# Split weights at drawn places in their buffers, and a narrower array of shifted columns

## The chip, the cores and the metric

The kernel runs on one core of one Trainium2 chip, in one launch. The metric is device time in microseconds. The kernel before was timed three times: 2295.11, 2295.64 and 2296.51 us, a median of 2295.64 us. Lines of the profile name the engines: PE is TensorE (matmuls), PEld its weight loads, DVE is VectorE, ACT is ScalarE, POOL is GpSimd, and SP is the engine that issues most DMAs.

## The reference

Two layers of a decoder trunk on one sequence of 256 tokens with 2048 channels, in float32. Each layer has a token mixer (layer 0 a causal convolution module, layer 1 stick-breaking attention with 16 heads) and a gated feed-forward part with a causal convolution of width 3. Every part is normalised and modulated by shift, scale and gate, which are products of the conditioning vector with a weight matrix of its own:

```python
def ada_ln(c, w, b):
    mod = jax.nn.silu(c) @ w + b
    shift, scale, gate = jnp.split(mod, 3, axis=-1)
    return shift[:, None, :], scale[:, None, :], gate[:, None, :]
...
def conv_ffn(h, up_w, dw_w, dw_b, down_w):
    u = causal_depthwise_conv(h @ up_w, dw_w, dw_b)
    gt, val = jnp.split(u, 2, axis=-1)
    return (jax.nn.silu(gt) * val) @ down_w
...
    for i in range(DEPTH):
        j = i // N_MIXERS
        shift, scale, gate = ada_ln(c, mix_mod_w[i], mix_mod_b[i])
        h = rms_norm(x, mix_norm_g[i]) * (1.0 + scale) + shift
        if i % N_MIXERS == 0:
            y = conformer_conv_module(h, cv_pw1_w[j], cv_pw1_b[j], cv_dw_w[j], cv_dw_b[j],
                                      cv_ln_g[j], cv_ln_b[j], cv_pw2_w[j], cv_pw2_b[j])
        else:
            y = stick_breaking_mixer(h, sb_qkv_w[j], sb_o_w[j])
        x = x + gate * y
        shift, scale, gate = ada_ln(c, ffn_mod_w[i], ffn_mod_b[i])
        h = rms_norm(x, ffn_norm_g[i]) * (1.0 + scale) + shift
        x = x + gate * conv_ffn(h, ffn_up_w[i], ffn_dw_w[i], ffn_dw_b[i], ffn_down_w[i])
    return rms_norm(x, final_norm_g)
```

`D_FF` is 5632, so the two up and down projections, the four products of the attention (q, k, v, o) and the two of the convolution module (pw1, pw2) are nearly all of the arithmetic.

## The kernel before

Activations are kept transposed: channels on the 128 partitions, the 256 tokens along the free dimension, 16 tiles for 2048 channels. All weight matrices but the modulation's come in pieces of 8 blocks of 128x128 (`PB`, `PW` = 1024 columns, 4096 bytes in a partition), in the order in which a table (`plan`) uses the blocks.

**Split weights.** Except for pw1, a product is made in the faster float32r type with each factor split into a high part and a low rest. A piece is loaded by SP into one of 6 `raw` buffers (`load_next`, L231), ACT copies it with rounding into `wh` (L241), and DVE subtracts that from the piece into `wl` (L245). `wh` and `wl` have 4 buffers each in the pool `wsplit`, one behind the other, and three pieces are split ahead of the one in use. Each 128x128 block is 512 bytes in a partition.

**Products.** `gemm` walks through the pieces. For each block it issues either three matmuls of 256 columns, high with high, high with low, low with high (L301, L302, L303), or two: the high weights against high and low part of the activations side by side, 512 columns (L296), and the low weights against the high part, 256 columns (L297). The second way is taken where `both` is given: in all of the second layer's up projections but the first four tiles, in the attention's o and its q and k but the first four tiles, and in the down projections, save for the last of their 16 output tiles. In `v_product` the roles change: the activations are the weights that are loaded, and the split weights stream through, 512 columns in each of L1184 to L1186.

**Where activations lie.** `h_tiles` places the 16 tiles of h 2304 bytes apart, the low part 1056 bytes behind the high part (a gap of 32 bytes). `halved` does so for the other split activations by the table `PAIRS`: the second layer's g like h, the first layer's g and o 2048 bytes apart and without a gap, z 2112 bytes apart with a gap of 32 bytes. The first tile can be moved by an offset (`ahead`).

**Order.** Each engine executes its instructions in program order. The order of pieces comes from `plan`; the work of ACT and DVE between the matmuls is placed by rates per piece (`RATES`). The change edits `split_next`, and two places of the first part that take it up: `load_rows` (L556, three of its row tiles lie in buffers of `wsplit`) and `hot`.

**The array of shifted columns.** In the first part, `mod_rows` makes some of the modulation vectors with rows of the matrix as the moving operand. The weights there are 32 columns of `hot`, all zero but one: `hot` holds silu(c) at column 31 of 63 for each of 16 tiles (L525 to L527), and the slice `31 - i : 63 - i` puts it at column `i` (L585). `i` is 0 to 3.

Of the kernel before, what the change touches and what calls it, by code (L numbers as in the profile page):

```python
# [2 lines left out]

# [7 lines left out]
F32 = mybir.dt.float32  # L11
F32R = mybir.dt.float32r
# [4 lines left out]
P = 128  # L17
PB = 8
PW = PB * P
# [99 lines left out]
def hybrid_trunk(ctx: ExitStack, tc: tile.TileContext, cfg: Cfg, io: dict):  # L119
    nc = tc.nc  # L120
    D, T, H = cfg.D, cfg.T, cfg.H
    KD, KF, CW, FW = cfg.KD, cfg.KF, cfg.CW, cfg.FW
# [7 lines left out]
    w_pool = ctx.enter_context(tc.tile_pool(name="wsplit", bufs=4))  # L130
# [5 lines left out]
    def psum_acc():  # L136
        return acc.tile([P, 512], F32, name="ps")
# [4 lines left out]
    def psum_b():  # L142
        return aux.tile([P, 512], F32, name="auxb", bufs=2)
# [22 lines left out]
    def pc(name, i0=0, n=None):  # L166
        if name in cfg.ccols:
            t, (a, b) = cpar["t"], cfg.ccols[name]
        else:
            t, (a, b) = par, cfg.cols[name]  # L170
        return t[:, a:b] if n is None else t[:, a + i0:a + i0 + n]
# [50 lines left out]
    def load(src, dst):  # L222
        tc.keep_in_program_order(nc.sync.dma_start(dst, src))

    def load_next():
# [4 lines left out]
        load(io["w_" + name][i, :, :n], v[:, :n])  # L230
        raws.append((blocks, v, n))  # L231

    def split_next(later=False):

        blocks, v, n = raws[len(parts)]
        if stream[len(parts)][0] == "pw1":
            parts.append((blocks, v, None))
            return
        wh = w_pool.tile([P, PW], F32R, name="wh")
        wl = w_pool.tile([P, PW], F32R, name="wl")  # L240
        nc.scalar.copy(wh[:, :n], v[:, :n])  # L241
        parts.append((blocks, wh, wl))

        def low():
            nc.vector.tensor_tensor(wl[:, :n], v[:, :n], wh[:, :n].bitcast(F32), op=ALU.subtract)  # L245

        if later:
            return low
        low()

    def pieces(name):

        for i in range(-(-len(cfg.plans[name]) // PB)):
            at = look["at"]
            assert stream[at] == (name, i)
            look["at"] += 1
            while len(raws) < min(len(stream), at + 1 + look["load"]):
                load_next()
            while len(parts) < min(len(stream), at + 1 + look["split"]):
                split_next()  # L260
            yield parts[at]
# [242 lines left out]
    with ExitStack() as cv:  # L504
        cpool = cv.enter_context(tc.tile_pool(name="conv", bufs=1))
# [11 lines left out]
        for k in range(0, D, 512):  # L517
            ps = psum_acc()
# [3 lines left out]

        cs = cpool.tile([P, KD], F32, name="cs")
        nc.scalar.activation(cs, pc("c"), AF.Silu)
        hot = cpool.tile([P, KD, 63], F32, name="hot")  # L525
        nc.vector.memset(hot, 0.0)
        nc.vector.tensor_copy(hot[:, :, 31:32], cs.unsqueeze(2))  # L527

        def gate_done():
            nc.vector.tensor_tensor(gb, modv["mix0"][:, 2 * KD:3 * KD], pc("pw2_b"), op=ALU.mult)  # L530
# [13 lines left out]
        def load_rows(most=1):  # L544

            while row_chunks and most:
                n = nrow["n"]
                near = n < nrow["near"]
                home = row_homes[n] if near else ("zmm"[n % 3] if n < 8 * KD // 4 else "zm"[n % 2]) if "z" in cpar else "m"
                cap = {"m": 3 if near else 1 + (n < 8 * KD // 4), "r": MORE_ROWS, "w": SPLIT_ROWS, "z": 1}[home]  # L550
                if sum(t[1] == home for t in row_tiles) >= cap:
                    break
                m, c, k0 = row_chunks.pop(0)
                src = io["mr_" + m][mr_at[m].index(c), :, k0 * 512:(k0 + 4) * 512]
                if home == "w":
                    v = [w_pool.tile([P, PW], F32R, name=x).bitcast(F32) for x in ("wh", "wl")]  # L556
                    for i in range(2):
                        load(src[:, i * PW:(i + 1) * PW], v[i])
                    v = [v[g // 2][:, g % 2 * 512:(g % 2 + 1) * 512] for g in range(4)]
                else:  # L560
                    v = (cpool2.tile([P, 4 * 512], F32, name="mrow", bufs=MORE_ROWS) if home == "r" else
                         cpar["z"].tile([P, 4 * 512], F32, name="zrow") if home == "z" else
                         mpool.tile([P, 4 * 512], F32, name="mraw"))
                    if "z" in cpar:
                        nc.gpsimd.dma_start(v, src)
                    else:
                        load(src, v)
                    v = [v[:, g * 512:(g + 1) * 512] for g in range(4)]
                row_tiles.append((v, home))
                nrow["n"] += 1  # L570
                most -= 1

        def mod_rows():

            for m, c0, n, done in rows_of:
                ps = (psum_acc if m == "ffn0" and c0 else psum_a)() if n else None
                for i in range(n):  # L580
                    for k0 in range(0, KD, 4):
                        v = row_tiles.pop(0)[0]
                        first, last = i == 0 and k0 == 0, i == n - 1 and k0 + 4 >= KD
                        for g in range(4):
                            nc.tensor.matmul(ps[32 * g:32 * g + 32, :], hot[:, k0 + g, 31 - i:63 - i],  # L585
                                             v[g], start=first, stop=last,
                                             tile_position=(0, 32 * g))
                        load_rows()
                        if later and nrow["bias"]:
                            later.pop(0)()  # L590
                        if last:
                            rows = cpool.tile([P, 512], F32, name="rows")
                            nc.scalar.copy(rows, ps)
                        else:
                            yield
                if n:
                    ps2 = psum_b()

                    def turn(rows=rows, n=n, ps2=ps2):
                        for b in range(4):  # L600
                            nc.tensor.matmul(ps2[:, b * n:(b + 1) * n], rows[:, b * P:(b + 1) * P], sel[:, :n],
                                             start=True, stop=True)

                    def bias(m=m, c0=c0, n=n, ps2=ps2, done=done):
                        o = modv[m][:, c0 * 4:(c0 + n) * 4].rearrange("p (c b) -> p b c", b=4)
                        v = pc(bname[m], c0 * 4, n * 4).rearrange("p (c b) -> p b c", b=4)
                        nc.vector.tensor_tensor(o, ps2[:, :4 * n].rearrange("p (b c) -> p b c", b=4), v, op=ALU.add)
                        done()

                    later.extend([turn, bias])  # L610
                    yield
            while later:
                later.pop(0)()
                yield

        def mods0():
            first = 4 * cfg.rows0
            todo, loaded = list(range(first, KD)), []

            def reduce_loaded():  # L620
                while loaded:
                    on = last_of(nc.vector.engine)
                    mod_reduce("ffn0", *loaded.pop(0))
                    behind(on)

            def load_one():
                nb = todo.pop(0)
                loaded.append((nb, mod_load("ffn0", nb)))

            for _ in mod_rows():  # L630
                reduce_loaded()
                yield
                if ("ffn0", 1) in have and todo:
                    load_one()
                    yield
            while todo:
                load_one()
                yield
                reduce_loaded()
            reduce_loaded()  # L640
            if first < KD:
                mod_sum("ffn0", first, KD - first)
            have.add(("ffn0", 0))
            yield
# [172 lines left out]
        for i in range(KD * HEAD // PB):  # L817
            pw1_piece(next(pw1))
            if (i + 1) % (HEAD // PB) == 0:
                start_tile()  # L820
        fill.append(mods0())
        load_rows(1)
        look["load"], look["split"] = 5, 0
        load(io["params"], par)
# [23 lines left out]
        for c in range(KD + 1):  # L848
# [12 lines left out]
            for s in range(nd):  # L861
# [17 lines left out]
                if c == KD and s == 0:  # L879
                    low = split_next(later=True)  # L880
# [347 lines left out]
    for h in range(2):  # L1228
        t = slice(h * HT, (h + 1) * HT)
        nc.vector.reciprocal(rs[:, t], std[:, t])  # L1230
        v = mpool.tile([P, D], F32, name="mraw")[:, :KD * HT].rearrange("p (k t) -> p k t", k=KD)
# [105 lines left out]
def build(nc, cfg, arrays):  # L1337
    io = {k: nc.dram_tensor(f"in_{k}", v.shape, F32, kind="ExternalInput").ap() for k, v in arrays.items()}
    io["out"] = nc.dram_tensor("out_0", (cfg.KD // 2, P, 2 * cfg.T), F32, kind="ExternalOutput").ap()
    with tile.TileContext(nc) as tc:  # L1340
        hybrid_trunk(tc, cfg, io)
# [19 lines left out]
```

## Time and profile before

| | us |
|---|---|
| median of three runs | 2295.64 |
| lowest and highest | 2295.11, 2296.51 |
| the profiled execution | 2295.03 |
| its span, first to last instruction | 2293.3 |
| TensorE from the first large product of split weights to the end of the last down projection | 284 to 2280 |

The stages of the profiled execution, by the first matmul of each: pw1 from 24 us, pw2 from 284 us, the first feed-forward part from 407 us (up projection until 670, down until 784, up until 1029, down until 1155), attention until 1545, the second feed-forward part until 2280, in the same halves. The matmuls' records overlap, since they are pipelined: the time that one costs is the distance from its start to that of the next, not its duration. A row of the timeline begins with the start and the duration in us. A row of the windows view begins with the stretch and its length, then gives for each engine the busy time and the number of instructions, then the granted clock, the DMA share and GB/s; with a line given it counts that line alone. In the rows of groups the busy time of all and the mean of one in ns stand behind the count.

### The profile page before, as it was taken

How to read it: one execution, taken by the hardware profiler on the slowest of the kernel's cores; microseconds unless marked ns; L12 is line 12 of the kernel's file. 1: busy time of each engine (PE TensorE's matmuls, PEld its weight loads, DVE VectorE, ACT ScalarE, POOL GpSimd, SP SyncE). 2: the span in 40 equal slices, each digit the busy share in tenths (PEclk: the TensorE clock that was granted, in tenths of full speed). 3: DMA queues.
4: the chain of work that ended last, by engine and by line, in shares of the span. 5: the costliest groups of instructions: out<-in, count | busy, mean ns of one | idle time of the engine just before them, and what ended most of it. 6: DMA issues, size and time to landing. Idle time of an engine off the chain costs nothing.

```text
span 2293.3 us, 37838 instructions
## 1 busy us (share of the span) xinstructions
PE 2259.4 (99%) x14466; PEld 2013.9 (88%) x14466; DVE 1791.2 (78%) x2502; ACT 1218.4 (53%) x1930; POOL 411.6 (18%) x535
## 2 busy tenths in 40 slices
PE   7999999999999999999999999999999999999997
PEld 5888678999998999998898888889888888888887
DVE  7689968989998899999975655778899755777654
ACT  2056655755544455555465555657555544555553
POOL 4058713200002100003421100122000010000031
PEclk9999999999999999999999999999999999999999
DMA  9988798789899989888765555566787665666663
GB/s 396 417 337 305 272 364 348 279 299 336 334 332 347 347 316 331 338 325 306 291 192 161 167 174 174 166 192 232 238 286 283 194 192 185 192 192 185 193 191 111
DMA packets 139144, 603.16 MB, mean 263 GB/s; under 512 B 15441, under 2 KB 15569, under 8 KB 115153
## 3 DMA queue, kind: packets, MB, share of 16 engines
q1 hardware_dynamic: 120242, 464.42, 57.8%
q0 software_dynamic: 18720, 136.32, 16.2%
q8 instruction: 113, 1.85, 0.3%
q14 instruction: 69, 0.57, 0.1%
HBM read 598.58 MB, written 2.10 MB: 262 GB/s over the span
## 4 chain that ended last, share of the span: by engine, by line
PE 87%; DVE 6%; DMA 4%; ACT 1%; issue 1%; POOL 0%; DVEq 0%; SPq 0%; ACTq 0%; POOLq 0%
PE ps L296 33%; PE ps L297 17%; PE ps L302 9%; PE ps L301 9%; PE ps L303 9%; PE ps L694 5%; DMA mraw<-in_mt_mix 3%; DVE mraw L335 3%; DVE wl L245 1%; PE ps L1185 1%; PE ps L1184 1%; PE ps L1186 1%; PE ps L585 1%; DMA mraw<-in_mt_ffn 1%; DMA raw<-in_w_pw 1%
## 5 line engine op out<-in xcount | busy, mean ns | idle before, releaser
L245 DVE TENSOR_TENSOR wl<-raw,wh 128x1024 fp32r<-128x1024 f32 x688 | 848.1, 1239 | 298.7 <-ACT wh L241 294.5
L241 ACT CAST wh<-raw 128x1024 fp32r<-128x1024 f32 x688 | 719.5, 1048 | 663.2 <-PE ps L296 279.6
L296 PE MATMUL ps<-h,wh 128*128 128x512 f32 x1760 | 613.5, 394 | 0.0
L297 PE MATMUL ps<-h,wl 128*128 128x256 f32 x1760 | 488.8, 278 | 0.0
L296 PE MATMUL ps<-g,wh 128*128 128x512 f32 x1320 | 458.1, 392 | 0.0
L303 PE MATMUL ps<-h,wl 128*128 128x256 f32 (+1 forms) x1504 | 423.4, 281 | 0.0
L302 PE MATMUL ps<-h,wh 128*128 128x256 f32 (+1 forms) x1504 | 423.2, 281 | 0.0
L301 PE MATMUL ps<-h,wh 128*128 128x256 f32 (+1 forms) x1504 | 419.8, 279 | 0.0
L296 PEld LDWEIGHTS ps<-h,wh 128*128 128x128 f32 x1760 | 330.4, 188 | 76.3
L335 DVE CUSTOM_DVE_ANT_0 mraw<-mraw,csr 128x2048 f32<-128x2048 f32 x152 | 350.1, 2304 | 32.1 <-DMA mraw<-in_mt_mix 28.6
L297 PE MATMUL ps<-g,wl 128*128 128x256 f32 x1320 | 369.9, 280 | 2.3 <-DVE wl L245 2.2
L297 PEld LDWEIGHTS ps<-h,wl 128*128 128x128 f32 x1760 | 330.5, 188 | 0.2
L296 PEld LDWEIGHTS ps<-g,wh 128*128 128x128 f32 x1320 | 247.8, 188 | 54.7
L301 PEld LDWEIGHTS ps<-h,wh 128*128 128x128 f32 x1504 | 284.2, 189 | 0.1
L303 PEld LDWEIGHTS ps<-h,wl 128*128 128x128 f32 x1504 | 283.0, 188 | 0.4
L302 PEld LDWEIGHTS ps<-h,wh 128*128 128x128 f32 x1504 | 283.1, 188 | 0.1
L297 PEld LDWEIGHTS ps<-g,wl 128*128 128x128 f32 x1320 | 248.6, 188 | 4.2 <-DVE wl L245 4.2
L694 PE MATMUL ps<-h,raw 128*128 128x256 f32 x832 | 188.8, 382 | 0.0
L694 PEld LDWEIGHTS ps<-h,raw 128*128 128x128 f32 x832 | 157.8, 191 | 28.3 <-issue 6.7
L1025 POOL TENSOR_TENSOR x<-x,t 128x256 f32<-128x256 f32 x56 | 70.5, 1260 | 526.8 <-ACT t L1024 526.7
L1003 DVE SCALAR_TENSOR_TENSOR t<-t,par 128x254 f32<-128x254 f32 (+1 forms) x184 | 88.7, 482 | 46.6 <-ACT t L1000 43.7
L734 DVE SCALAR_TENSOR_TENSOR auxb<-u,cpar,auxb 128x256 f32<-128x256 f32 x297 | 121.6, 482 | 4.5 <-ACT auxb L718 3.8
(271 smaller groups left out, 2739.7 us busy)
## 6 DMA issues: line engine op xcount, KB each, us to landing
raw<-in_w_down SPq DMA_DIRECT2D x176, 512.0 KB, 4.2
mraw<-in_mt_ffn POOLq DMA_DIRECT2D x64, 1024.0 KB, 5.8
raw<-in_w_pw SPq DMA_DIRECT2D x96, 512.0 KB, 8.1
mraw<-in_mt_mix POOLq DMA_DIRECT2D x48, 1024.0 KB, 7.7
raw<-in_w_up01b SPq DMA_DIRECT2D x84, 512.0 KB, 6.3
raw<-in_w_up11b SPq DMA_DIRECT2D x84, 512.0 KB, 3.6
raw<-in_w_up00b SPq DMA_DIRECT2D x80, 512.0 KB, 5.7
raw<-in_w_up10b SPq DMA_DIRECT2D x80, 512.0 KB, 4.7
```

What stands on the lines that cost most here:

```text
L241: nc.scalar.copy(wh[:, :n], v[:, :n])
L245: nc.vector.tensor_tensor(wl[:, :n], v[:, :n], wh[:, :n].bitcast(F32), op=ALU.subtract)
L296: nc.tensor.matmul(o, wh[:, c], both[kt], start=first, stop=False, skip_group_check=True)
L297: nc.tensor.matmul(o[:, :T], wl[:, c], xh[kt], start=False, stop=left[nb] == 0, skip_group_check=True)
L301: nc.tensor.matmul(o, wh[:, c], xh[kt], start=first, stop=False, skip_group_check=halves > 0)
L302: nc.tensor.matmul(o, wh[:, c], xl[kt], start=False, stop=False, skip_group_check=halves > 0)
L303: nc.tensor.matmul(o, wl[:, c], xh[kt], start=False, stop=left[nb] == 0, skip_group_check=halves > 0)
L335: nc.vector.tensor_tensor_reduce(out=v, in0=v, in1=csr, scale=1.0, scalar=0.0, op0=ALU.mult, op1=ALU.add, accum_out=macc[:, nb:nb + 1])
L694: nc.tensor.matmul(banks[j][:, nb // KD * T:(nb // KD + 1) * T], w[:, b * P:(b + 1) * P], hf[kt], start=first, stop=left[j] == 0, skip_gro ...
L734: nc.vector.scalar_tensor_tensor(conv_ps[j], us[j % UBUFS][:, k:k + T], tap(j, k), conv_ps[j], op0=ALU.mult, op1=ALU.add)
L1003: nc.vector.scalar_tensor_tensor(y[:, s:], ps[:, :T - s], w(k), y[:, s:], op0=ALU.mult, op1=ALU.add)
L1025: nc.gpsimd.tensor_tensor(xs[nb], xs[nb], t, op=ALU.add)
```

## The change

The buffers of `wh` and `wl` become 56 columns (224 bytes) longer, and each piece starts in its buffer at an offset that is drawn: a multiple of 4 columns, 16 bytes, from 0 to 224 bytes, high and low part apart. The draws come from a generator with a fixed seed, so they are the same in each build. The blocks' order, the copies and the subtractions stay. The row tiles that borrow these buffers start at their beginning, as before. `hot` holds its column at place 3 of 35, which is enough for `i` from 0 to 3; it gives back as many bytes (16 x 28 x 4 = 1792) as the longer buffers take (8 x 224 = 1792).

What lies behind the pool `wsplit` in a partition moves by 1792 bytes, 7 x 256: the tiles of g and o among it, but not h, which lies ahead. What is allocated behind `hot` while it is there (z among it) stays where it was.

```diff
+import random
...
+    place = random.Random(1)
+
     def split_next(later=False):
...
-        wh = w_pool.tile([P, PW], F32R, name="wh")
-        wl = w_pool.tile([P, PW], F32R, name="wl")
+        wh, wl = (w_pool.tile([P, PW + 56], F32R, name=x) for x in ("wh", "wl"))
+        at = 4 * place.randrange(56 // 4 + 1)
+        wh = wh[:, at:at + PW]
+        at = 4 * place.randrange(56 // 4 + 1)
+        wl = wl[:, at:at + PW]
         nc.scalar.copy(wh[:, :n], v[:, :n])
         parts.append((blocks, wh, wl))
...
-        hot = cpool.tile([P, KD, 63], F32, name="hot")
+        hot = cpool.tile([P, KD, 35], F32, name="hot")
         nc.vector.memset(hot, 0.0)
-        nc.vector.tensor_copy(hot[:, :, 31:32], cs.unsqueeze(2))
+        nc.vector.tensor_copy(hot[:, :, 3:4], cs.unsqueeze(2))
...
-                    v = [w_pool.tile([P, PW], F32R, name=x).bitcast(F32) for x in ("wh", "wl")]
+                    v = [w_pool.tile([P, PW + 56], F32R, name=x)[:, :PW].bitcast(F32) for x in ("wh", "wl")]
...
-                            nc.tensor.matmul(ps[32 * g:32 * g + 32, :], hot[:, k0 + g, 31 - i:63 - i],
+                            nc.tensor.matmul(ps[32 * g:32 * g + 32, :], hot[:, k0 + g, 3 - i:35 - i],
```

## The prediction

> **What bounds the kernel now.** I read the busy shares first, then the waits of TensorE, then the chain that ended last.
>
> ```profile
> PE 2259.4 (99%) x14466; PEld 2013.9 (88%) x14466; DVE 1791.2 (78%) x2502; ACT 1218.4 (53%) x1930; POOL 411.6 (18%) x535
> PEclk9999999999999999999999999999999999999999
> PE 87%; DVE 6%; DMA 4%; ACT 1%; issue 1%; POOL 0%; DVEq 0%; SPq 0%; ACTq 0%; POOLq 0%
> ```
>
> TensorE is busy 99% of the span at the full granted clock and carries 87% of the chain. A busy share alone says little for pipelined matmuls, so I asked for the waits of the matmuls and of the weight loads from 450 to 2280 us.
>
> ```profile
> PE ps L297 <- DVE wl L245: 2.2, 4, 0.7
> ...
> PEld ps L297 <- DVE wl L245: 4.2, 6, 1.0
> ```
>
> The largest wait of either is 4.2 us in 1830 us. So from 450 us on nothing is late for TensorE, and the time of the kernel is the number of matmuls times the distance between their starts. The counts, from the groups of matmuls kept apart by shape (mean ns behind the busy us); they are the same in both kernels:
>
> ```profile
> L296 PE MATMUL ps<-h,wh 128*128 128x512 f32 x1760 | 613.5, 394 | 0.0
> L296 PE MATMUL ps<-g,wh 128*128 128x512 f32 x1320 | 458.1, 392 | 0.0
> L296 PE MATMUL ps<-o,wh 128*128 128x512 f32 x256 | 89.5, 392 | 0.0
> L301 PE MATMUL ps<-h,wh 128*128 128x256 f32 x1312 | 364.7, 278 | 0.0
> L302 PE MATMUL ps<-h,wh 128*128 128x256 f32 x1312 | 368.7, 281 | 0.0
> L303 PE MATMUL ps<-h,wl 128*128 128x256 f32 x1312 | 368.6, 281 | 0.0
> L301 PE MATMUL ps<-h,wh 128*128 128x258 f32 x192 | 55.0, 287 | 0.0
> L302 PE MATMUL ps<-h,wh 128*128 128x258 f32 x192 | 54.5, 284 | 0.0
> L303 PE MATMUL ps<-h,wl 128*128 128x258 f32 x192 | 54.8, 285 | 0.0
> ```
>
> I call L296 (512 columns) with its L297 (256 columns) a pair, and L301, L302, L303 (256 columns each) a triple. Both stream 768 columns; the triple loads weights three times, the pair twice. There are 1760 + 1320 + 256 pairs in these rows and 32 more whose output lies in the other banks, 3368 in all, and 1312 + 32 = 1344 triples on h of 256 columns.
>
> A matmul's record is longer than the distance to the next, so the distances come from the starts. First and last L296 of a stretch of pairs on g, and how many there are in it:
>
> ```profile
> 1809.71 0.39 PE L296 MATMUL ps<-g,wh 128*128 128x512 f32 x1
> 1909.89 0.39 PE L296 MATMUL ps<-g,wh 128*128 128x512 f32 x1
> ...
> 1810.00:1910.00 100.00, 100.00 (x290) 54.16 (x289) 1.00 0.62 191
> ```
>
> 100.18 us for 289 steps: **346.6 ns a pair**. The same for triples on h (L301, 567 of them):
>
> ```profile
> 449.78 0.28 PE L301 MATMUL ps<-h,wh 128*128 128x256 f32 x1
> 649.77 0.28 PE L301 MATMUL ps<-h,wh 128*128 128x256 f32 x1
> ...
> 450.00:650.00 200.00, 157.36 (x567) 106.88 (x566) 1.00 0.88 324
> ```
>
> 199.99 us for 566 steps: **353.3 ns a triple**. Pairs on the first layer's g, which lies differently (below):
>
> ```profile
> 679.62 0.39 PE L296 MATMUL ps<-g,wh 128*128 128x512 f32 x1
> 779.81 0.39 PE L296 MATMUL ps<-g,wh 128*128 128x512 f32 x1
> ...
> 680.00:780.00 100.00, 100.00 (x290) 54.11 (x289) 1.00 0.92 342
> ```
>
> 100.19 / 289 is 346.7 ns, the same. Two more kinds of triple, on g at the end of the first down projection (21 steps) and on z at the end of pw2 (16 steps):
>
> ```profile
> 784.20 0.28 PE L303 MATMUL ps<-g,wl 128*128 128x256 f32 x1
> 791.55 0.28 PE L303 MATMUL ps<-g,wl 128*128 128x256 f32 x1
> ...
> 401.47 0.28 PE L303 MATMUL ps<-z,wl 128*128 128x256 f32 x1
> 407.07 0.28 PE L303 MATMUL ps<-z,wl 128*128 128x256 f32 x1
> ```
>
> 7.35 / 21 and 5.60 / 16: **350.0 ns** both times. These triples have the same columns, the same weights' place and the same engine as those on h; only the place of the moving operand differs, and 3.3 ns of 353 come with it. So places matter, by about 1%, and this is the whole lever of the change.
>
> **The places, before and after.** Before, every block of split weights starts at the same place modulo 256 bytes (the pieces step 4096 bytes, the blocks 512). Let the distance be the moving operand's address minus its weights', modulo 256. Tiles of h and of the second layer's g step by a multiple of 256, so their high part is always at distance 128 and their low part at 160: pairs 346.6, triples 353.3. The first layer's g and all of o are at distance 32 in both parts: triples 350.0. Tiles of z step by 2112 bytes, 64 more than a multiple of 256, so they pass through four distances in turn: 350.0 as their mean. After, the pieces' bases step 4320 bytes and each draws 0 to 224 bytes in steps of 16. Counted over the 1312 split pieces of the changed program, each of the 16 distances in steps of 16 comes 59 to 115 times; 719 pieces (55%) lie at a multiple of 32, as all did before, and 593 (45%) at an odd multiple of 16, which no row of before shows. The order of instructions is the same, row for row, on all five engines; one MEMSET gets narrower.
>
> **The sum, term by term.**
>
> Pairs: 3368. They stand at 346.6 at both distances tried, the lowest rate in the kernel. The nearest dear row is the triple on h, 6.7 ns more for the same 768 columns; the nearest cheap one is their own. Five kinds of work are seen (pairs at two distances, triples at 32, at the four of z and at 128/160) and one of them is dear, so I let one piece in four fall to the dear rate: 6.7 / 4 = 1.7 ns on the mean, 3368 x 1.7 = +5.7 us. Ends: 0, and 3368 x 6.7 = +22.6 us.
>
> Triples on h: 1344. They hold the dear distance now and can only keep it or leave it. Three in four to the rate of z: 1344 x 3.3 x 0.75 = -3.3 us. Ends: 0 and -4.4 us.
>
> Products for v (moving operand and weights change places there, 128 of each line with the other banks) and the triples of 258 columns:
>
> ```profile
> L1184 PE MATMUL auxb<-wh,h 128*128 128x512 f32 x32 | 12.5, 392 | 0.0
> L1185 PE MATMUL ps<-wl,h 128*128 128x512 f32 x96 | 38.3, 399 | 0.0
> L1186 PE MATMUL ps<-wh,h 128*128 128x512 f32 x96 | 37.9, 394 | 0.0
> ```
>
> Equal shapes, 392 to 399 ns: if all came to 392, 9 ns x 128 = -1.2 us; if all to 399, 12 ns x 128 = +1.5 us. The 258-column triples sum to 856 ns in the rows above against 840 for 256 columns; six more columns at 353.3 / 768 ns are 2.8 ns, so 13 ns may be their place: 192 x 13 = -2.5 us at most. I take half of both gains, -1.9 us.
>
> ACT's copy and DVE's subtraction write and read the moved pieces:
>
> ```profile
> L245 DVE TENSOR_TENSOR wl<-raw,wh 128x1024 fp32r<-128x1024 f32 x688 | 848.1, 1239 | 298.7 <-ACT wh L241 294.5
> L241 ACT CAST wh<-raw 128x1024 fp32r<-128x1024 f32 x688 | 719.5, 1048 | 663.2 <-PE ps L296 279.6 <-PE ps L302 205.9 <-issue 112.4
> ```
>
> All their operands stood at one place modulo 4096, so no row says what another place costs. TensorE's lead hides a change of some per cent either way: in the fullest stage DVE is busy
>
> ```profile
> 800.00:1020.00 220.00, 220.00 (x1870) 220.00 (x1869) 204.71 (x258) 113.36 (x156) 16.41 (x31) 1.00 0.88 326
> ...
> 800.00:1020.00 220.00, 93.75 (x78) 1.00 0.88 326
> ```
>
> 204.71 of 220 us, 93.75 of them in L245 (second row), so 15.3 us are free and L245 can lengthen by 16% before DVE is the bound. I take 0.
>
> The narrow `hot` array:
>
> ```profile
> 1.25 0.90 DVE L526 MEMSET hot<- 128x1008 f32 x1 [0.16 <-issue]
> 5.58 7.31 DVE L405 TENSOR_TENSOR sumsq<-sumsq,t 128x256 f32<-128x256 f32 x14 [3.43 <-ACT t L401]
> ```
>
> 560 columns for 1008 take 0.5 us for 0.90, and DVE then waits 3.43 us for ACT anyway: 0.
>
> Sum: 5.7 - 3.3 - 1.9 = +0.5 us on 2293.3 us of span and the 1.7 us around it (the profiled execution took 2295.03): 2295.5. That execution is 0.6 us under the median of the runs, so **2296 us**, no change that can be told. A measurement of this kernel tells about 0.2%, 4.6 us, from none.
>
> The Trainium skill speaks against any effect: SBUF — State Buffer, "Who interferes with whom", gives TensorE two independent read ports and says that it waits for no one, and its remark on cachelines ("Door 1") makes 16 bytes the line, so that every draw starts on a line. By it the sum would be 0 and the time 2295.6. The rows disagree with the strong form of it: 353.3 against 350.0 ns with nothing but places different. It stays as a rival below.
>
> **The rivals.**
>
> *The pairs lose their rate (slower).* Place: L296 and L297 from 670 us on. If the 346.6 is a rate that holds only at the two distances they stand at, and others give what z gives as a mean over four, 350.0, they cost 3368 x 3.4 = +11.5 us, with the triples' gain 2302 us; if others give 353.3, +22.6 less 5 is 2313 us. For it: pairs were only seen at two distances, and 45% of the draws are of a kind not seen. Against it: the two distances differ by 96 bytes and give one rate, and z holds 350.0 over all of its four. It decides from a mean pair of 346.6 + (4.6 + 5.2) / 3368 us, 349.5 ns, on. Chance 0.33.
>
> *Most places are cheap (faster).* All pairs stay, all triples on h come to 350.0, v and the 258 columns to their cheap ends: -4.4 - 1.2 - 2.5 = -8.1 us, 2287 us. For it: four of the five kinds are at the low rate for their count of weight loads. Against it: every draw must miss the dear distance. Chance 0.23.
>
> *The change does nothing (independent ports).* Then what differs between h and z is the moving operand's own place, not its distance to the weights, and the moved weights change no rate: 2295.6 us. Against it the v rows: 392, 399 and 394 ns with the moving pieces at one place and only the h part different. Chance 0.13.
>
> *DVE or ACT slows.* At 25% on L245, 23.4 us in that stage against 15.3 free, 8.1 us; in the two stages of this kind some 17 us: 2312. Chance 0.04; nothing speaks for it but that it isn't shown.
>
> **How the numbers follow.** The forecast's own mixture has 0.27, with the independent ports 0.40 within 0.2%; the pairs and DVE give 0.37 for slower, the cheap places 0.23 for faster. The range reaches from the cheap end, 2287, to the dear end of the pairs with a little of DVE, 2315.
>
> **What would show it.** Starts of L296 over 1810 to 1910 us: 346.6 or up to 349 for the forecast, 350 and over for the first rival. Starts of L301 over 450 to 650 us: about 351 for the forecast, 353.3 for independent ports. Within a stretch the distance between pairs should now change from piece to piece, 8 pairs at a time, where before it didn't. L245 and L241 should keep 1239 and 1048 ns. I am wrong if distances at odd multiples of 16 have a rate of their own outside 346 to 353, or if TensorE begins to wait for `wl`.

## The result: 11 us slower, in the steps from pair to pair

| | before | after |
|---|---|---|
| median | 2295.64 us (2293.35 to 2301.74, 5 runs) | 2307.06 us (2305.22 to 2307.29, 5 runs) |
| ratio to before | | 1.0045, interval 1.003 to 1.006 |
| the profiled execution, and its span | 2295.03, 2293.3 | 2305.22, 2303.5 |

The changed kernel is slower by 0.45% of the time: outside the 0.2% that can be told from no change, inside the range of the prediction, and 11 us above its point. (The ratio is formed between runs that stand beside each other, so it is not quite the quotient of the medians.)

In the changed kernel the lines of the matmuls are six further down: a pair is L302 and L303, a triple L307 to L309, ACT's copy L247 and DVE's subtraction L251. From its page, the busy shares, the engines' shares of the chain that ended last, and the two groups that write and read the moved pieces:

```profile
PE 2270.5 (99%) x14466; PEld 2020.4 (88%) x14466; DVE 1791.4 (78%) x2502; ACT 1220.1 (53%) x1930; POOL 410.3 (18%) x535
...
PE 86%; DVE 7%; DMA 4%; ACT 1%; issue 1%; POOL 0%; DVEq 0%; SPq 0%; ACTq 0%; POOLq 0%
...
L251 DVE TENSOR_TENSOR wl<-raw,wh 128x1024 fp32r<-128x1024 f32 x688 | 849.0, 1240 | 308.2 <-ACT wh L247 305.9
L247 ACT CAST wh<-raw 128x1024 fp32r<-128x1024 f32 x688 | 719.6, 1048 | 673.0 <-PE ps L302 287.5
```

TensorE is still busy 99% of the span. DVE and ACT take 1240 and 1048 ns for a piece as before (1239, 1048). They merely stand idle longer, DVE 308.2 us before L251 in place of 298.7. The largest waits of the matmuls and of the weight loads from 450 us on:

```profile
PE ps L303 <- DVE wl L251: 1.7, 3, 0.7
...
PEld ps L303 <- DVE wl L251: 3.7, 6, 1.0
```

1.7 and 3.7 us, where they were 2.2 and 4.2: nothing comes late for TensorE. So what was lost lies in the matmuls themselves. Their groups by shape, for pairs and for triples on h:

```profile
L302 PE MATMUL ps<-h,wh 128*128 128x512 f32 x1760 | 619.7, 396 | 0.0
L302 PE MATMUL ps<-g,wh 128*128 128x512 f32 x1320 | 462.6, 395 | 0.0
L302 PE MATMUL ps<-o,wh 128*128 128x512 f32 x256 | 90.2, 396 | 0.0
...
L307 PE MATMUL ps<-h,wh 128*128 128x256 f32 x1312 | 368.0, 281 | 0.0
```

The counts are the same. The records of the pairs are 2 to 4 ns longer than before (394, 392 and 392), that of L307 3 ns (278). What they cost is read from the starts, in the stretches of the prediction. L302 on the second layer's g, with the window of that line:

```profile
1809.70 0.40 PE L302 MATMUL ps<-g,wh 128*128 128x512 f32 x1
1909.79 0.40 PE L302 MATMUL ps<-g,wh 128*128 128x512 f32 x1
...
1810.00:1910.00 100.00, 100.00 (x287) 53.61 (x286) 1.00 0.62 191
```

100.09 us for 286 steps are **350.0 ns a pair** (346.6 before, 290 of them in the same 100 us). On h, and then the triples on h (L307):

```profile
1599.93 0.40 PE L302 MATMUL ps<-h,wh 128*128 128x512 f32 x1
1799.89 0.40 PE L302 MATMUL ps<-h,wh 128*128 128x512 f32 x1
...
1600.00:1800.00 200.00, 200.00 (x572) 107.23 (x572) 1.00 0.73 256
```

```profile
449.77 0.28 PE L307 MATMUL ps<-h,wh 128*128 128x256 f32 x1
649.66 0.28 PE L307 MATMUL ps<-h,wh 128*128 128x256 f32 x1
...
450.00:650.00 200.00, 158.25 (x565) 106.34 (x565) 1.00 0.88 323
```

199.96 / 571 is 350.2 ns a pair; 199.89 / 564 is 354.4 ns a triple (353.3 before). The granted clock is 1.00 in all three windows, as before. Summed over all matmuls, from start to next start, after less before:

| | number | us |
|---|---|---|
| pairs on h | 1792 | +6.1 |
| pairs on the second layer's g | 660 | +2.5 |
| pairs on the first layer's g | 660 | +1.5 |
| pairs on o | 256 | +0.7 |
| triples on h, 256 columns | 1344 | +1.6 |
| triples on g; on z | | +0.3; -1.8 |
| triples of 258 columns; products for v | 192; 128 lines | -0.2; -0.5 |
| all of the matmuls | | +10.2 |

The spans differ by the same 10.2 us, so the table is all of the difference between the two traces, and the pairs are +10.8 of it. The -1.8 us on z do not come from places: in the trace of the kernel before, the granted clock was 0.50 for 3.4 us from 398.0 us on, while z was multiplied, and a triple took 640 ns there; the changed kernel's trace has no such stretch. TensorE in the same microsecond, before and after:

```profile
399.00:400.00 1.00, 1.00 (x7) 0.50 1.03 410
...
399.00:400.00 1.00, 1.00 (x11) 1.00 1.04 414
```

Of the eleven experiments' traces below, six have this stretch and five have not, whatever their places. Without it the two traces here would differ by some 12 us (an estimate: 10.2 and 1.8).

Two neighbouring pieces show how the loss of the pairs is spread, eight pairs each; rows of the timeline for the second and the last pair of the first piece, and for the first and the last of the next:

```profile
1361.97 0.40 PE L302 MATMUL ps<-h,wh 128*128 128x512 f32 x1
...
1364.17 0.40 PE L302 MATMUL ps<-h,wh 128*128 128x512 f32 x1
1364.53 0.39 PE L302 MATMUL ps<-h,wh 128*128 128x512 f32 x1
...
1366.99 0.40 PE L302 MATMUL ps<-h,wh 128*128 128x512 f32 x1
```

Six steps of the first piece take 2.20 us, 367 ns each; seven of the next take 2.46 us, 351 ns. Within these two the steps agree within some ns (elsewhere they can alternate, at 96/192 below between 345 and 365 ns), and at the boundary the rate jumps. Over all 418 pieces with at least five undisturbed steps between pairs the mean is 350.2 ns, from 341.9 to 366.7; 69 pieces, one in six, are still within half a ns of the old 346.7, or below. From here "distance" means addresses, and the time from start to start is a step or a rate. I give two distances as x/y: the address of the moving operand less that of the high weights, and less that of the low weights, both modulo 256 bytes. The first of these pieces stands at 0/32, the second at 32/96; before, h stood at 128/128 throughout.

### The profile page after: what moved, and what is told of

It is laid out like the page before. It is cut to its first block, busy times and chain, and to the rows that moved or that the text cites. A ratio compares the mean times of both kernels' runs of the same rounds, so it can differ in the third digit from the quotient of the medians.

```text
span 2303.5 us, 37838 instructions
## 1 busy us (share of the span) xinstructions
PE 2270.5 (99%) x14466; PEld 2020.4 (88%) x14466; DVE 1791.4 (78%) x2502; ACT 1220.1 (53%) x1930; POOL 410.3 (18%) x535
## 4 chain that ended last, share of the span: by engine, by line
PE 86%; DVE 7%; DMA 4%; ACT 1%; issue 1%; POOL 0%; DVEq 0%; SPq 0%; ACTq 0%; POOLq 0%
PE ps L302 32%; PE ps L303 16%; PE ps L307 9%; PE ps L308 9%; PE ps L309 9%; PE ps L700 5%; DMA mraw<-in_mt_mix 3%; DVE mraw L341 3%; DVE wl L251 2%; PE ps L1191 1%; PE ps L1192 1%; PE ps L1190 1%; PE ps L591 1%; DMA raw<-in_w_pw 1%; DMA mraw<-in_mt_ffn 1%
## 5 line engine op out<-in xcount | busy, mean ns | idle before, releaser
L251 DVE TENSOR_TENSOR wl<-raw,wh 128x1024 fp32r<-128x1024 f32 x688 | 849.0, 1240 | 308.2 <-ACT wh L247 305.9
L247 ACT CAST wh<-raw 128x1024 fp32r<-128x1024 f32 x688 | 719.6, 1048 | 673.0 <-PE ps L302 287.5
L302 PE MATMUL ps<-h,wh 128*128 128x512 f32 x1760 | 619.7, 396 | 0.0
L303 PE MATMUL ps<-h,wl 128*128 128x256 f32 x1760 | 492.8, 280 | 0.0
L302 PE MATMUL ps<-g,wh 128*128 128x512 f32 x1320 | 462.6, 395 | 0.0
L307 PE MATMUL ps<-h,wh 128*128 128x256 f32 (+1 forms) x1504 | 422.9, 281 | 0.0
L309 PE MATMUL ps<-h,wl 128*128 128x256 f32 (+1 forms) x1504 | 422.6, 281 | 0.0
L302 PEld LDWEIGHTS ps<-h,wh 128*128 128x128 f32 x1760 | 330.6, 188 | 77.0
L303 PE MATMUL ps<-g,wl 128*128 128x256 f32 x1320 | 370.1, 280 | 1.9 <-DVE wl L251 1.7
L303 PEld LDWEIGHTS ps<-h,wl 128*128 128x128 f32 x1760 | 331.8, 189 | 0.2
L302 PEld LDWEIGHTS ps<-g,wh 128*128 128x128 f32 x1320 | 247.9, 188 | 58.1
L309 PEld LDWEIGHTS ps<-h,wl 128*128 128x128 f32 x1504 | 283.5, 188 | 0.5 <-DVE wl L251 0.2
L307 PEld LDWEIGHTS ps<-h,wh 128*128 128x128 f32 x1504 | 283.5, 189 | 0.1
L303 PEld LDWEIGHTS ps<-g,wl 128*128 128x128 f32 x1320 | 248.6, 188 | 3.7 <-DVE wl L251 3.7
```

The lines of the kernel that those rows point to most:

```text
L302: nc.tensor.matmul(o, wh[:, c], both[kt], start=first, stop=False, skip_group_check=True)
L303: nc.tensor.matmul(o[:, :T], wl[:, c], xh[kt], start=False, stop=left[nb] == 0, skip_group_check=True)
L307: nc.tensor.matmul(o, wh[:, c], xh[kt], start=first, stop=False, skip_group_check=halves > 0)
L309: nc.tensor.matmul(o, wl[:, c], xh[kt], start=False, stop=left[nb] == 0, skip_group_check=halves > 0)
```

## The experiments

Theory at this point: the rate of a pair or triple follows from these two distances. Rivals: it is the draw itself, the change of place from piece to piece, that costs; it is the longer buffers and the narrower `hot`; it is where a piece lies, whatever the moving operand's address.

Most kernels below keep the change's longer buffers and narrow `hot`, and set the places by hand. Bases of the buffers step by 4320 bytes, 32 less than a multiple of 256, and `k` is the number of the buffer (the tuple in `split_pair` is the order in which the pool hands them out), so that `at, to = 0, 0` gives the distances of before. `at` and `to` are in columns of 4 bytes: 8 of them lower a distance by 32 bytes.

```diff
+    held = {"n": 0}
+
+    def split_pair():
+        held["n"] += 1
+        return [w_pool.tile([P, PW + 56], F32R, name=x) for x in ("wh", "wl")], (0, 3, 2, 1, 0, 2, 1, 3)[(held["n"] - 1) % 4 + 4 * (held["n"] > 24)]
...
+        (wh, wl), k = split_pair()
+        at, to = 0, 0
+        at, to = (at + 8 * k) % 64, (to + 8 * k + 32) % 64
+        wh, wl = wh[:, at:at + PW], wl[:, to:to + PW]
```

**The change's layout at the old distances** (the edit just shown).

> Buffers 56 columns longer and the narrow array as in the change, but the offset of each piece is chosen by its buffer so that every distance (moving operand's address minus weights' address, modulo 256 bytes) is what it was before; piece to piece the place in the buffer still differs by up to 224 bytes. Theory 'distance': the rate of TensorE follows the two distances alone, so pairs start every 346.7 ns and triples on h every 353.3 ns as before, 2295.6 us. Rival 'layout': longer buffers, the shift of what lies behind them, or the narrow array cost the time, so some 2306 us as in the change.

2295.10 us (2293.42 to 2303.12, 12 runs) against 2295.40 (23 runs): 0.9993, interval 0.998 to 1.0006. Window of its pairs (L304 there):

```profile
1600.00:1800.00 200.00, 200.00 (x579) 108.31 (x578) 1.00 0.75 259
```

579 in the window as before (579; 572 after the change). (The count takes in records that reach into the window from ahead of it; rates in ns are read from the starts.) The buffers, `hot` and everything that moved behind them cost nothing.

**Weights and activations moved together.** The tile of h that comes first is moved by 64 bytes, and so is all that is allocated behind it, the weights too; the distances stay.

```diff
-H_AHEAD, H_SIZE, H_LOW, H_LAST = 32, 576, 264, 544
+H_AHEAD, H_SIZE, H_LOW, H_LAST = 48, 576, 264, 544
...
```

This kernel and the one with h moved alone are the kernel before with the narrow `hot`, whose lines are left out here.

> The kernel before with the narrow array, and the offset ahead of the first tile of h raised from 32 to 48 columns: h, the raw and the split weights and all behind them move by the same 64 bytes, so each has another place of its own modulo 256, and every distance stays. Theory 'distance': pairs every 346.7 ns, 2295.6 us. Rival 'own place' (the weights' or the activations' own place modulo 256 sets the rate, and the earlier runs moved it together with the distance): another rate, by the mean of the changed kernel 350.2 ns for 3368 pairs, some 2306 us.

2295.24 us (2293.87 to 2295.54, 11 runs) against 2295.01: 1.0001, interval 0.9993 to 1.001. The pairs (L296) number 578 in the same window, and pairs and triples on h keep their rates. So a place of its own doesn't set them, as far as one shift of 64 bytes tells. Only the triples of 258 columns ran otherwise: 15 of their 24 pieces at 353.3 ns, where before all had stood at 362 to 366. Five of them did so, too, in the kernel with the pairs alone drawn (below), which leaves their places as they were, so the shift isn't needed for it.

**One dear place, nothing drawn.** Pairs on h and on the second layer's g (I call these two-part pairs, since a gap lies between their halves) stand at 96/192 throughout.

```diff
+PLACES = {"qk0a": (0, 0), "qk": (8, 48), "up10b": (8, 48), "up11": (8, 48), "down1": (8, 48)}
...
-        at, to = 0, 0
+        at, to = next((v for x, v in PLACES.items() if stream[len(parts)][0].startswith(x)), (0, 0))
```

> As same_distances, but all pieces of the pairs in two parts (on h and on the second layer's g, 2452 pairs) lie at one fixed pair of distances, 96 to the high and 192 to the low weights, at which five pieces of the changed kernel started pairs every 352.8 ns. No draws. Theory 'distance': 6.1 ns more for each of 2452 pairs, +15 us, 2310.6 us, slower than the change although nothing varies. Rival 'variation' (the change costs time because places differ from piece to piece): 2295.6 us.

2310.81 us (2309.3 to 2311.38, 5 runs): 1.0051, interval 1.0035 to 1.0067. The window of its pairs on h, and their group:

```profile
1600.00:1800.00 200.00, 200.00 (x567) 106.24 (x566) 1.00 0.73 255
...
L305 PE MATMUL ps<-h,wh 128*128 128x512 f32 x1760 | 624.9, 400 | 0.0
```

567 in 200 us are 353.3 ns a pair, more than with the draws, and the records grow to 400 ns. A loss needs no draw.

**The activations moved, the weights left.** h moves by 160 bytes, to 32/32; the pool grows by 256, so that all behind it keeps its distance.

```diff
-H_AHEAD, H_SIZE, H_LOW, H_LAST = 32, 576, 264, 544
+H_AHEAD, H_SIZE, H_LOW, H_LAST = 72, 576, 264, 568
...
```

> The kernel before with the narrow array, and the tiles of h alone moved by 160 bytes against the weights (72 columns ahead of the first, 24 more behind the last, so that all else moves by 256): the weights keep their places modulo 256, and the distances of h become 32/32. Three pieces of the changed kernel at 32/32 had pairs every 352.2 ns and triples every 353.5. Theory 'distance': 1792 pairs on h x 5.5 ns = +10 us, triples on h unchanged, some 2306 us; what v and the 258 columns do there isn't known (1 or 2 us). Rival 'own place of the weights': 2295.6 us.

2302.06 us (2300.21 to 2302.41, 7 runs): 1.0029, interval 1.0018 to 1.0039. Windows of the pairs (L296), first on h, then on g:

```profile
1600.00:1800.00 200.00, 200.00 (x567) 106.26 (x567) 1.00 0.74 255
1815.00:1915.00 100.00, 100.00 (x290) 54.23 (x289) 1.00 0.62 191
```

Of the pairs only those on h slow down, to 353.3 ns here and 351.3 as a mean: +8.0 us. The mean hides two rates at one place: in the second layer's up projection 83 pieces of the first half ran at 353.3 and the 84 of the second at 349.5. g, not moved, keeps its 290. Here the weights lie where they lay, so their own place can't be the cause; in the kernel with one dear place h lay where it lay, so its own place can't be either; with both moved together nothing happened to the pairs. What is left is the distance. The size was less than I expected. The first layer's g stands at 32/32 too and ran at 346.7: it has no gap between its halves, so the two distances aren't all that counts.

**The drawn places, for a part of the pieces.** With the draws of the change for the pieces of pairs alone, and in a second kernel for all other pieces alone. The generator has the same seed and is asked as often, so a drawn piece gets the very place that it has in the changed kernel.

```diff
+DRAWN = ("down", "o", "qk0b", "qk1", "qk2", "qk3", "up10b", "up11")
...
+        at, to = 8 * k, (8 * k + 32) % 64
+        draw = 4 * place.randrange(15), 4 * place.randrange(15)
+        if stream[len(parts)][0].startswith(DRAWN):
+            at, to = draw
+        wh, wl = wh[:, at:at + PW], wl[:, to:to + PW]
```

(`if not` in the second.)

> The draws of the change for the pieces of pairs alone (down projections, o, q and k, the second layer's up projections, save the first four tiles); all others keep the distances of before. Theory: the pairs carry the whole loss, 3.3 ns on 3368 pairs, +11 us, 2306.6 us.

> The complement: the draws of the change for all pieces but those of pairs, which keep the distances of before. Theory: triples on h 1.1 ns dearer on the mean (+1.5 us), v and the 258 columns a little cheaper (-0.7 us): no change, 2296.4 us. The prediction's own step (triples gain 3.3 us) would give 2291 us.

Pairs alone: 2305.9 us (2304.43 to 2308.14, 5 runs), 1.0049, interval 1.0036 to 1.0062. The rest alone: 2296.23 us (2294.6 to 2302.76, 12 runs), 1.0006, interval 0.9998 to 1.0015. So the pairs carry the change's loss, and the draws give the triples nothing. The rates repeat, too: 402 of the 418 pieces of pairs ran within 1 ns of what the same piece took in the changed kernel, and in the second kernel all 168 pieces of triples on h did. The spread between pieces belongs to the program, not to the single execution. The triples on h in the second kernel (L315):

```profile
450.00:650.00 200.00, 158.27 (x565) 106.31 (x565) 1.00 0.88 323
```

565 as in the changed kernel, 567 before: 354.5 ns, +1.6 us in all. A third thing stands in that trace, taken in the longest of its 12 runs, 2302.76 us. Its two-part pairs (L310) were not moved, and yet:

```profile
1600.00:1800.00 200.00, 200.00 (x567) 106.23 (x566) 1.00 0.73 254
1815.00:1915.00 100.00, 100.00 (x284) 53.12 (x284) 1.00 0.60 187
1960.00:2140.00 180.00, 180.00 (x520) 97.52 (x520) 1.00 0.62 189
```

567 and 284 are 353.3 ns, at 128/128; 520 in 180 us are the old 346.7. By the starts, the high rate held for 122 pieces in a row, from a stall at 1579 us, the only wait of the matmuls from 1560 us to 2280,

```profile
PE auxb L311 <- DVE wl L259: 0.6, 1, 0.6
```

to the triples that end the first half of the down projection at 1925 us; behind them the low one held to the end. 122 x 8 x 6.6 ns are 6.4 us, about what this run took over the median of the others. **One pair of distances can have two rates**, each held for hundreds of us.

**Cheap places, nothing drawn.** From the pieces of the changed kernel that ran fastest: two-part pairs at 16/0, the first layer's triples on h at 192/128, the pairs on the first layer's g and on o at 64/0; the low weights of v move by 128 bytes, the first tiles' triples to 32/0.

```diff
+PLACES = {"up00a": (24, 32), "up10a": (24, 32), "qk0a": (24, 32), "up0": (48, 0), "down0": (56, 8), "o": (56, 8),
+          "v": (0, 32), "qk": (28, 32), "up1": (28, 32), "down1": (28, 32)}
```

> As same_distances, with fixed distances by kind of product, each taken from the cheapest pieces of the changed kernel's trace: pairs in one run (first layer's g, o) at 64/0, there 340 to 342 ns for 346.7; pairs in two parts at 16/0, there 345.3 for 346.7; triples on h at 192/128, there 347.5 for 353.3; v at 128/0, there 687 for 700; the 258 columns at 32/0, there 356.6 for 363.1. Theory 'distance': -6, -3.4, -8, -1.7 and -1.2 us, some 2275 us, faster than both. Rival 'variation': 2295.6 us, as these places are fixed as well. Rival 'layout': some 2306 us.

2280.68 us (2279.16 to 2282.47, 4 runs): **0.9922, interval 0.9904 to 0.9939**, better than both kernels. Windows of its triples on h (L311) and of its two-part pairs (L306):

```profile
450.00:650.00 200.00, 159.23 (x578) 109.03 (x577) 1.00 0.90 331
...
1600.00:1800.00 200.00, 200.00 (x581) 108.75 (x581) 1.00 0.75 260
```

578 triples are 346.7 ns (567 before), -8.8 us in all; 581 pairs are 345.2 ns, -3.9 us. For these triples only the high weights have another distance than before, by 64 bytes, so the effect doesn't simply repeat every 64 bytes. The 5 us that miss my expectation are at 64/0. Rows of the timeline, on the first layer's g, first and last of two stretches of even steps:

```profile
1073.11 0.39 PE L306 MATMUL ps<-g,wh 128*128 128x512 f32 x1
...
1075.15 0.39 PE L306 MATMUL ps<-g,wh 128*128 128x512 f32 x1
1075.74 0.40 PE L306 MATMUL ps<-g,wh 128*128 128x512 f32 x1
...
1079.94 0.40 PE L306 MATMUL ps<-g,wh 128*128 128x512 f32 x1
```

Six steps in 2.04 us are 340 ns; then one step of 590 ns, with a stall in it; then twelve in 4.20 us, 350 ns. The operands' distances are the same on both sides of the stall. Most of g ran at 350 and lost 0.9 us where I expected -4.4; o ran at 340.

**Three places drawn in turn.** Two-part pairs at 128/128, 224/192 or 96/64, all of which had shown 346.7 to 347.3 ns in the changed kernel or before (128/128 had one piece of 350).

```diff
+CHEAP = ((0, 0), (40, 48), (8, 16))
+DRAWN = ("qk0b", "qk1", "qk2", "qk3", "up10b", "up11", "down1")
...
+        at, to = place.choice(CHEAP) if stream[len(parts)][0].startswith(DRAWN) else (0, 0)
```

> As same_distances, but the pieces of the pairs in two parts are drawn among three places whose distances are cheap in the changed kernel's trace: 128/128 (346.7 ns), 224/192 (346.7) and 96/64 (347.2). Theory 'distance': +0.2 ns on the mean, 2296 us. Rival 'variation': the rate is lost because places differ from piece to piece, 350 ns for 2452 pairs, +8 us, 2304 us.

2301.1 us (2299.27 to 2302.61, 11 runs): 1.0012, interval 1.0002 to 1.0022, between the two expectations. Split by place, 128/128 ran at 347.3 ns, 96/64 at 346.7 and 224/192 at 352.8. Nearly all of the loss is at one place. That left open whether this place is dear, or becomes so when the piece before stood elsewhere.

**That place alone, nothing drawn**, and **two places drawn** that are cheap when fixed:

```diff
-PLACES = {"qk0a": (0, 0), "qk": (8, 48), "up10b": (8, 48), "up11": (8, 48), "down1": (8, 48)}
+PLACES = {"qk0a": (0, 0), "qk": (40, 48), "up10b": (40, 48), "up11": (40, 48), "down1": (40, 48)}
```

```diff
-CHEAP = ((0, 0), (40, 48), (8, 16))
+CHEAP = ((0, 0), (28, 32))
```

> All two-part pairs (on h and on the second layer's g, some 2450) stand at distances 224/192 throughout, the one of the three drawn places at which the drawn kernel lost (352.8 ns there); nothing varies. If 224/192 is a dear place by itself, they run at about 352.8 ns: 2450 x 6.1 = +15 us, about 2310 us. If its dear rate is only taken up when the piece before stood elsewhere (variation), they run at 346.7, as three pieces of the changed kernel did there: about 2295 us.

> Two-part pairs drawn piece by piece between 128/128 (346.7 ns when fixed) and 16/0 (345.2 when fixed). If the rate belongs to the place and a change of place costs nothing: the mean is 346.0, 2450 x -0.7 = -1.8 us, about 2293.5 us. If changing from piece to piece sends places to their second, slower rate (350 or more in half of the pieces): +4 us or more, 2299 and up.

The first: 2303.13 us (2301.3 to 2311.37, 10 runs), 1.0034, interval 1.0019 to 1.0049, neither of the two. Its two-part pairs (L305), with nothing varied:

```profile
1600.00:1800.00 200.00, 200.00 (x578) 108.31 (x578) 1.00 0.75 259
...
1960.00:2140.00 180.00, 180.00 (x511) 95.64 (x510) 1.00 0.62 187
```

578 in 200 us are 346.7 ns; 511 in 180 us are 353. By the starts, the low rate began behind the first pairs of the up projection, at 1578 us, and ended with the triples at 1917 us: the same two places at which the kernel with the rest drawn changed its rate, but the other way round. In all, 140 pieces ran at 347 and 153 at 353. So 224/192 has both rates without any draw.

The second: 2295.81 us (2292.14 to 2301.29, 10 runs), 1.0002, interval 0.999 to 1.0014. Its profiled run, of 2292.14 us, has 347.0 ns at 128/128 and 345.6 at 16/0, what these places have when fixed. In it the change of place cost next to nothing (6 of its 154 pieces at 128/128 ran at 353). The median lies between the two expectations: the longer runs, up to 9 us more, have no trace, and may hold the second rate.

**The cheap places once more**, with the first layer's g left at 32/32 (346.7) instead of 64/0:

```diff
-PLACES = {"up00a": (24, 32), "up10a": (24, 32), "qk0a": (24, 32), "up0": (48, 0), "down0": (56, 8), "o": (56, 8),
+PLACES = {"up00a": (24, 32), "up10a": (24, 32), "qk0a": (24, 32), "up0": (48, 0), "o": (56, 8),
```

> As cheap_fixed, but the first layer's g stays at 32/32, where it ran at 346.7 ns, and does not go to 64/0, where it had a rate of 350 for most of its pieces and of 340 for some; o stays at 64/0. By the rates seen: 0.9 us less than cheap_fixed, about 2279.8 us. If o, which ran at 340 there, settles at 350 this time: 256 x 10 ns more, about 2282 us.

2282.75 us (2279.29 to 2284.32, 4 runs): 0.9935, interval 0.9916 to 0.9955. Neither reason was it: o kept its 340 ns. The triples on h (L311), in the gate's and the value's half of the up projection:

```profile
450.00:650.00 200.00, 158.67 (x562) 105.38 (x561) 1.00 0.87 321
830.00:1000.00 170.00, 135.31 (x491) 92.74 (x491) 1.00 0.92 341
```

562 in 200 us are 356 ns, where the kernel before it had 578 at the same place; 491 in 170 us are 346.7. That is +6.5 us. The profiled run was the longest of the four, and the two kernels can't be told apart by their intervals.

## Why the prediction was right and wrong

**What bounds.** Right: from 450 us on TensorE waited for next to nothing, and the loss is in the steps between matmuls. The forecast, no change that can be told, was wrong. The range held because its dear end was drawn for the rival that came about.

**The pairs, +5.7 us by "one piece in four to the dear rate".** The term had its sign and its mechanism and was mis-sized: +10.8 us. The step that failed is the count "five kinds of work are seen and one of them is dear". It took five kinds at their places for a sample of places. The pairs had been seen at two places only, with 346.7 ns both times, and that is the low end of what a pair does: in the changed kernel one piece in six is there, the mean is 350.2, and 28 of 418 pieces are even above 353.5. The mean went half of the way from 346.6 to 353.3, not a quarter.

**The triples on h, -3.3 us by "three in four to the rate of z".** Wrong in sign: +1.6 us. I called 353.3 the dear rate because z and g had 350.0. It was near the average: over drawn places the triples on h came to 354.5, and with the draws for them alone they came to that too. The lower rate does exist, 346.7 at 192/128, but few draws come near it.

**The v products and the 258 columns, -1.9 us.** The sign held, the size was -0.7.

**ACT, DVE, `hot`, 0.** Held: 1048 and 1240 ns, no new wait; layout alone gave 0.9993.

**The rivals.** What happened is the first one, the pairs losing their rate, in its milder form: 350.0 as z has, +11.5 us, and it decides from 349.5 ns. Measured were 350.2 ns and +10.8; without the triples' gain that the forecast had added, 2307 comes out and not 2302. That a mean of 350.2 stands beside its 350.0 is luck, though. It had taken 350.0 from the last 16 steps on z, while 24 of the 32 pieces of z before the change ran at 352 to 357 ns, and the drawn pairs spread from 341.9 to 366.7. Its objection, that two distances 96 bytes apart gave one rate, weighed too much in my chances. Odd multiples of 16, which I had set apart, aren't the cause: their mean is 350.0 ns, that of multiples of 32 is 350.3. (The 1312 "split pieces" that the prediction counts are the high and low parts of 656 pieces.) Independent ports meant that moved weights change no rate. The kernel with one dear place rules that out: there the weights alone moved, and the pairs went from 346.7 to 353.3 ns. The rule of the Trainium skill (SBUF — State Buffer, "Who interferes with whom"), by which TensorE's two read ports are independent and it waits for no one, does not account for these runs: the same pairs with the same granted clock took 345.2 ns at 16/0 and 353.3 at 96/192, in kernels of 2280.68 and 2310.81 us that differ in places alone. That the ports are the reason isn't shown.

**Shown, and still open.** Shown: a change of the distance between operands changes what a pair or a triple costs, the pairs carry the loss, and neither layout nor drawing as such does. The load of the DMA engines isn't the cause either: at 128/128 pairs took 346.7 ns at a DMA share of 0.75 and of 0.62. Open: what in the chip makes a distance dear. No run varied what the other engines read and write meanwhile. Since a place can have two rates, it is open too how much of the changed kernel's 350.2 ns is dear places, as 96/192 is (353.3 fixed, 352.7 to 353.0 in its five drawn pieces), and how much is second rates of cheap ones. The two distances explain about half of the spread between its pieces.

## What to carry to other kernels

Where TensorE is busy throughout and waits for nothing, look at the steps between starts of matmuls by family: equal shapes with unequal steps, no wait and the same granted clock point to addresses, and here fixed, chosen distances were worth 0.7 to 0.8% while drawn ones cost 0.45%. Before predicting from a few rates that a kernel shows, ask where they lie in the spread of all places: two equal good rates don't say that the next place is good. Time a place more than once, since it can have a second rate that a single profile doesn't show.

## What the runs showed of the hardware that was not expected

A steady stream of float32r matmuls has a rate that, as long as it holds, repeats to about 1 ns over a long stretch. It depends on the moving operand's address less the weights' modulo 256 bytes, and lay between 340 and 367 ns for the same 768 columns. At some distances there are two such rates: 340 and 350 at 64/0 without a gap, 346.7 and 353.3 at 128/128 and at 224/192, 350 and 353.3 at 32/32 on h, and for triples 346.7 and 356 at 192/128. Where the one changed for the other, there was a stall or other work in between, and the clock was granted in full on both sides. This would explain why single runs of the kernel before reached 2303.38 us where most took 2293 to 2296; that was not shown, since none of those runs has a trace.

In seven of the thirteen traces the granted clock fell to 0.50 for 3.4 us, near 398 us, and in six it did not; the traces don't show why.
